# Splitting mixer weights with casting and accumulating transfers instead of GpSimd

## The chip, the cores and the metric

The kernel runs on one core of a Trainium2 chip. The metric is the device time of one execution in microseconds (us); the time before is the median of three runs. The engines are named TensorE (PE; its weight loads PEld), VectorE (DVE), ScalarE (ACT), GpSimd (POOL) and SyncE (SP, which here only issues transfers). Each has its own in-order instruction queue, and they meet at semaphores.

## The reference

Two layers of a network over 256 latent tokens and 256 context tokens of width 1024, all in float32. Each layer is a half-step SwiGLU FFN, a token mixer and another half-step FFN, each with its own modulation, gate and LayerNorm. What matters here is the mixer:

```python
def token_mixer(h, hc, rope, p, ctx_out):
    (ca, cg, lx, lg, gqkv, gz, ga, gb, aq, ak, av, gates) = split_in(h @ p['w_in'])
    ...
    y_conv = conformer_conv(ca, cg, p)
    y_lru, y_lru_c = rglru_branch(lx, lx_c, lg, lg_c, p, ctx_out)
    y_gdn, y_gdn_c = gdn_branch(gqkv, gqkv_c, gz, gz_c, ga, ga_c, gb, gb_c, p, ctx_out)
    ...
    y_att = window_attention(q, k, v, kc, vc, p['att_sink'])

    def merge(y_a, y_b, y_c, y_d, gate_cols):
        gt = jax.nn.sigmoid(gate_cols).reshape(gate_cols.shape[:-1] + (N_BRANCH, D))
        mrg = gt[..., 0, :] * (y_a @ p['proj_conv'])
        mrg = mrg + gt[..., 1, :] * (y_b @ p['proj_lru'])
        mrg = mrg + gt[..., 2, :] * (y_c @ p['proj_gdn'])
        mrg = mrg + gt[..., 3, :] * (y_d @ p['proj_att'])
        return mrg @ p['w_out']
```

In the second (last) layer only the latent tokens are merged, so most of its projections have 256 columns in place of 512.

## The kernel before

Every large product is made of three TensorE products of rounded operands: a float32 value r is split into hi, which is r rounded to the format fp32r, and lo = r - hi, and w x is wh xh + wh xl + wl xh (`mm3`, lines 376 to 381). Weights come from HBM as tiles of 128 partitions by 1024 columns (0.5 MB), and `chunk` (line 98) splits each: SP issues the transfer into one of two buffers `wr`, ScalarE casts it into `wh` (line 120), and VectorE or GpSimd subtracts to make `wl` (line 121). There are three `wh` and three `wl` buffers; some weights go to other slots (F, G, Y, B) instead. In a G slot a weight is two halves with a cast and a subtraction each.

Who subtracts is given by `self.lo`, a string of letters through which successive weights cycle: P is GpSimd, D is VectorE. The mixer is a set of generators (GDN convolution, keys and values, scan, attention, conformer convolution, LRU, merges), and a string of letters per layer, `ORDER`, says which one takes its next step. Three capital letters in that string set `self.lo` (line 36):

```python
LO = {"P": "P", "D": "DP", "X": "D"}
```

In the first mixer P is set for most of the weights and "DP" from the merges on, and after the string `self.lo = "D" if last else "DP"` (line 1322) holds for the last merges and the output projection. In the second mixer P is set after the first letter and D after the string. A projection onto the mixer's inputs (`z`, line 542) takes one weight and 24 matmuls. A merge step (`merge`, line 1269) takes three weights: a projection tile, used in two halves of 12 matmuls, and a gate's tile (24 matmuls) ahead of each half.

The order of instructions on each queue is not the program's alone: the kernel is built by a planner (`schedule_with_timeline_sim=True`) that plays the program through with costs of its own and puts on each queue, by priority, what it thinks is ready. A transfer that GpSimd issues is an instruction in GpSimd's queue, and what is behind it waits until its semaphores allow it.

The lines that the prediction names: 120 and 121 the split of a weight, 127 the split of an activation (subtraction), 868 and 831 the GDN scan's multiplications on GpSimd, 864 and 877 its work on VectorE, 1107 the 31-tap convolution on VectorE, 1047 to 1068 the LRU, 1294 the merge's addition on GpSimd.

Of the kernel before, what the change touches and what calls it, by code (L numbers as in the profile page):

```python
# [12 lines left out]
F32 = mybir.dt.float32  # L13
F32R = mybir.dt.float32r
BF16 = mybir.dt.bfloat16
AF = mybir.ActivationFunctionType
ALU = mybir.AluOpType
P = 128
D = 1024
# [13 lines left out]
    0, 124, 128, 132, 136, 168, 176, 184, 192, 200, 296, 298, 300, 301, 309)  # L33
NEG = -1e30
N_CH = 16
LO = {"P": "P", "D": "DP", "X": "D"}
ORDER = (
    "eggePgegeggXgeggggggPgegggvggvggvggvgggggggaabgggabggzabababzabababllllggababababzababgllablglzbvvvvvccccvvccvccssssssssPssssssDmmllllmmllllsmmmmsmmmmmmmm",
    "gPggggeeeggecgggcgeggggeggccgvgvggvvggggccgagggggbaabgzggggvggabzvabgccggvabbabazbvvvvvzssssslssssssslllllsPssmmlllllsmmmllllmlmmmmmmmmmm",
# [10 lines left out]
class Net:  # L50
# [46 lines left out]

    def chunk(self, src, at=None, raw=None):
        nc = self.nc
        pool_lo = self.lo[self.n_ck % len(self.lo)] == "P"  # L100
        self.n_ck += 1
        if raw is None:
            raw = self.sb.tile([P, 1024], F32, tag="wr", bufs=2, name="wr")
            nc.sync.dma_start(raw, src)
        elif isinstance(raw, str):
            raw = self.slot(raw, name="raw")[:, :1024]
            nc.sync.dma_start(raw, src)
        if at == "G":
            hi, lo = ([self.G(F32R) for _ in range(2)] for _ in range(2))
            parts = [(hi[k], lo[k], raw[:, k * 512:(k + 1) * 512]) for k in range(2)]  # L110
        else:
            if at:
                w = self.slot(at, F32R, name="w" + at)
                hi, lo = w[:, :1024], w[:, 1024:]
            else:
                hi = self.sb.tile([P, 1024], F32R, tag="wh", bufs=3, name="wh")
                lo = self.sb.tile([P, 1024], F32R, tag="wl", bufs=3, name="wl")
            parts = [(hi, lo, raw)]
        for h, l, r in parts:
            nc.scalar.copy(h, r)  # L120
            (nc.gpsimd if pool_lo else nc.vector).tensor_sub(l, r, h.bitcast(F32))  # L121
        return hi, lo

    def split(self, hi, lo, src, pool_lo=True):
# [280 lines left out]
    def ffn(self, l, f, j, tiles, H, fill, after, start=None):  # L405
# [9 lines left out]
        def two(src, at=(None, None)):  # L415
            if lat:
                return self.pair(src, "Y", at)
            return [chunk(src[a], at[a]) for a in range(2)]

        for fi, (m0, m1) in enumerate(F_SPLIT):  # L420
# [48 lines left out]
            if fi < len(F_SPLIT) - 1:  # L469
                for dh in range(2):  # L470
                    ps = {t: self.ps("px" if t == 3 else "pm") for t in tiles}
                    ws = []
                    for i in range(n):
                        i0 = m0 // 2 + i
                        if i == n - 1 and not i % 2:
                            ws.append(chunk(src[dh][i]))
                        elif not i % 2:
                            ws += two(self.t["f2"][l, f, dh, i0:i0 + 2])
                        w = ws[i]
                        for t in tiles:  # L480
                            self.down_mm(ps[t], hid, t, n, i, w)
                        if fill and i % 2:
                            fill.pop(0)()
                    for t in tiles:
                        self.resid(t, dh, ps[t], ALPHA if fi == 0 else 1.0)
            else:
                while fill:
                    fill.pop(0)()
                ws = [[chunk(src[dh][i], at=DOWN_AT[dh][i]) for i in range(n)] for dh in range(2)]


# [41 lines left out]
        else:  # L533
            nc.vector.tensor_add(x, x, t1)

# [1 line left out]

    def z_mm(self, ps, w, H, c):
        for k in range(KD):
# [759 lines left out]
    def mixer(self, l, H, last, after):  # L1299
        nc = self.nc  # L1300
        tiles = (2, 3) if last else (0, 1, 2, 3)
        c = slice(256, 512) if last else slice(0, 512)
        self.vec = self.sb.tile([P, V_N], F32, tag="vec", bufs=1, name="vec")
        with self.tc.issue_after(self.mark):
            nc.scalar.dma_start(self.vec, self.t["vec"][l])
        self.l, self.inv = l, None
        self.ysp = [self.dr.tile([P, 4, 512], F32, tag=f"ysp{b}", bufs=1, name="ysp") for b in range(4)]
        for s in range(2):
            if not (last and s == 0):
                nc.sync.dma_start(self.xspill[s], self.x[s])  # L1310
        self.z_head(l, H, [Z_GK + h for h in range(4)] + [Z_AK if last else Z_GQ])
        S, extra = self.att_z(l, H, last)
        self.conv_init()
        self.gdn_init()
        st = dict(
            g=self.gdn(l, H, last), v=self.gdn_values(l, H, last), s=self.gdn_scan(last),
            e=(f() for f in extra), a=self.att(self.att_scores, S, tiles),
            b=self.att(self.att_values, S, tiles), z=(self.gdn_z(l, H, last, h) for h in range(4)),
            c=(x for i in range(4) for x in self.conv(l, H, last, i)), l=self.lru(l, H, last), m=self.merges(l, H, last, c))
        ws = {}  # L1320
        self.emit(st, ORDER[l], "gvezabclsm")
        self.lo = "D" if last else "DP"
        y = [None, None]
        if last:
            mh = [a.rearrange("p (k t) -> p k t", k=KD) for a in (self.F(F32R), self.F(F32R))]
            spots = SPOT
        else:
            spots = ("F", "F", "F", "F", "F", "G", "G", None)
        self.ju = self.T

        def fetch(n0, n1):
            for n in range(n0, n1):
                ws[n] = self.chunk(self.t["wo"][l, n // 4, n % 4], at=spots[n])

        def conv_out():
            y[0] = self.new_y()
            self.conv_norm(last, y[0])
            yield

        def gdn_out():  # L1340
            y[1] = self.new_y()
            for t in tiles:
                self.gdn_out(t, y[1])
                yield

        done = [0] * 4

        def merged(i):
            done[i] += 1
            if last and done[i] == 2:  # L1350
                self.mh_split(mh, i, c)

        def merge_conv():
            for i in range(4):
                yield from self.merge(l, 0, y[0], H, last, False, i, lambda: merged(i))

        def merge_gdn():
            for i in range(4):
                yield from self.merge(l, 2, y[1], H, last, False, i, lambda: merged(i))

        def fetches():
            for i in range(4 if last else 7):
                fetch(i, i + 1)
                yield

        self.emit(dict(n=conv_out(), o=gdn_out(), c=merge_conv(), g=merge_gdn(), f=fetches()), TAIL[l], "nocgf")
        if not last:
            mh = self.new_h()
            for i in range(4):
                self.mh_split(mh, i, c)  # L1370
        self.x = [None, None]
        for s in range(2):
            if not (last and s == 0):
                self.x[s] = self.Y(name="x")
                nc.sync.dma_start(self.x[s], self.xspill[s])
        self.gate_rows(l, 1, 0.5, (1,) if last else (0, 1))
        self.norm_rows(l, 1)
        fetch(4 if last else 7, 8)

        def mm(t, dh, sums):  # L1380
            ps = self.ps()
            with self.hold():
                for i in range(4):
                    self.wo_mm(ps, mh, t - 2 if last else t, i, ws[4 * dh + i])
            self.resid(t, dh, ps, ALPHA, sums)

        self.out_loop(tiles, mm, after)

    def emit(self, streams, order, rest):
        for ch in order:  # L1390
            if ch in LO:
                self.lo = LO[ch]
            else:
# [165 lines left out]
```

## Time and profile before

| | |
|---|---|
| median of 3 runs | 2820.98 us (2819.75 to 2821.17) |
| profiled execution | span 2816.3 us from first to last instruction, 37869 instructions |
| around the span, to the median | 4.7 us |
| TensorE busy | 2593.8 us, 92% |
| VectorE busy | 1955.0 us, 69% |
| ScalarE busy | 1093.3 us, 39% |
| GpSimd busy | 1008.0 us, 36% |
| moved by transfers | 396.99 MB, 141 GB/s on the mean; transfers issued by GpSimd 0.07 MB |

The profiled execution is one execution, and its own time is given by its span; the runs are timed without that profile. Busy times are of the whole span, and stages with different limits are mixed in them. The mean of a group of instructions mixes undisturbed and stretched ones. "Idle before" names what ended an engine's wait.

### The profile page before, as it was taken

How to read it: one execution, taken by the hardware profiler on the slowest of the kernel's cores; microseconds unless marked ns; L12 is line 12 of the kernel's file. 1: busy time of each engine (PE TensorE's matmuls, PEld its weight loads, DVE VectorE, ACT ScalarE, POOL GpSimd, SP SyncE). 2: the span in 40 equal slices, each digit the busy share in tenths (PEclk: the TensorE clock that was granted, in tenths of full speed). 3: DMA queues.
4: the chain of work that ended last, by engine and by line, in shares of the span. 5: the costliest groups of instructions: out<-in, count | busy, mean ns of one | idle time of the engine just before them, and what ended most of it. 6: DMA issues, size and time to landing. Idle time of an engine off the chain costs nothing.

```text
span 2816.3 us, 37869 instructions
## 1 busy us (share of the span) xinstructions
PE 2593.8 (92%) x14382; PEld 2174.2 (77%) x14382; DVE 1955.0 (69%) x3129; ACT 1093.3 (39%) x1995; POOL 1008.0 (36%) x691
## 2 busy tenths in 40 slices
PE   5999998998898999999999999999979878888898
PEld 3787877776777787878878888888867767688898
DVE  8695966678999834265969467623698898756455
ACT  3322235483332533353222442223536534344443
POOL 4323223222535344433232332323332278731221
PEclk9999999999999999999999999999989989999899
DMA  6554542234422343434545344423222534357353
GB/s 226 191 179 169 201 145 102 69 109 153 140 83 91 113 135 117 164 113 157 181 171 196 102 166 167 149 95 115 91 90 92 156 116 133 105 183 240 135 181 118
DMA packets 162216, 396.99 MB, mean 141 GB/s; under 512 B 28417, under 2 KB 68577, under 8 KB 161265
## 3 DMA queue, kind: packets, MB, share of 16 engines
q1 hardware_dynamic: 158114, 384.55, 40.9%
q10 hardware_dynamic: 3888, 9.96, 1.1%
q8 instruction: 113, 1.85, 0.3%
q14 instruction: 69, 0.57, 0.1%
q0 software_dynamic: 32, 0.07, 0.0%
HBM read 360.92 MB, written 33.60 MB: 140 GB/s over the span
## 4 chain that ended last, share of the span: by engine, by line
PE 34%; DVE 13%; issue 3%; DMA 2%; POOL 2%; ACT 2%; SPq 0%; POOLq 0%; ACTq 0%; DVEq 0%
PE pm L380 10%; PE pm L381 10%; PE pm L379 10%; DVE C L1107 2%; DVE G L572 1%; DVE junk L169 1%; DVE wl L121 1%; DVE G L864 1%; PE px L381 1%; PE px L380 1%; PE px L379 1%; DMA wr<-in_wo_dram 1%; DVE lru L1049 1%; DVE M L781 1%; PE pg L873 0%
## 5 line engine op out<-in xcount | busy, mean ns | idle before, releaser
L379 PE MATMUL pm<-h,wh 128*128 128x512 f32 (+1 forms) x2512 | 895.5, 358 | 36.6 <-ACT h L125 12.8
L381 PE MATMUL pm<-h,wl 128*128 128x512 f32 (+1 forms) x2512 | 890.9, 355 | 16.8 <-DVE wl L121 14.8
L380 PE MATMUL pm<-h,wh 128*128 128x512 f32 (+1 forms) x2512 | 892.0, 355 | 13.0 <-POOL h L127 6.7
L121 POOL TENSOR_TENSOR wl<-wr,wh 128x1024 fp32r<-128x1024 f32 x166 | 419.8, 2530 | 697.6 <-ACT wh L120 649.0
L120 ACT CAST wh<-wr 128x1024 fp32r<-128x1024 f32 x340 | 356.7, 1050 | 785.6 <-PE pm L380 275.2
L379 PEld LDWEIGHTS pm<-h,wh 128*128 128x128 f32 x2512 | 484.0, 193 | 109.1 <-ACT h L125 15.6
L381 PEld LDWEIGHTS pm<-h,wl 128*128 128x128 f32 x2512 | 484.8, 193 | 87.0 <-DVE wl L121 18.8
L380 PEld LDWEIGHTS pm<-h,wh 128*128 128x128 f32 x2512 | 485.1, 193 | 80.9 <-POOL h L127 10.1
L121 DVE TENSOR_TENSOR wl<-wr,wh 128x1024 fp32r<-128x1024 f32 x174 | 243.6, 1400 | 263.0 <-ACT wh L120 261.6
L169 DVE SCALAR_TENSOR_TENSOR junk<-wa,cb 128x1024 bf16<-128x1024 f32 x256 | 358.3, 1442 | 9.2 <-DMA wa<-in_adaw_dram 8.6
L127 POOL TENSOR_TENSOR F<-G,F 128x512 fp32r<-128x512 f32 (+1 forms) x94 | 139.4, 1483 | 426.2 <-ACT F L125 426.1
L1107 DVE SCALAR_TENSOR_TENSOR C<-C,vec 128x482 f32<-128x482 f32 (+29 forms) x240 | 208.2, 867 | 4.1 <-ACT C L1099 0.9
L380 PE MATMUL pm<-wl,F 128*128 128x512 f32 x368 | 145.5, 395 | 0.0
L379 PE MATMUL pm<-wh,F 128*128 128x512 f32 x368 | 145.4, 395 | 0.0
L381 PE MATMUL pm<-wh,F 128*128 128x512 f32 x368 | 144.1, 395 | 0.0
L393 DVE TENSOR_TENSOR G<-G,pm 128x512 f32<-128x512 f32 (+1 forms) x93 | 54.4, 585 | 125.9 <-PE pm L381 118.9
L121 DVE TENSOR_TENSOR wl<-raw,wh 128x1024 fp32r<-128x1024 f32 x61 | 75.0, 1231 | 63.6 <-ACT wh L120 63.6
L125 ACT CAST F<-G 128x512 fp32r<-128x512 f32 (+1 forms) x94 | 50.9, 542 | 154.1 <-DVE G L393 154.1
L868 POOL TENSOR_TENSOR wk<-wk,cd 128x512 f32<-128x512 f32 x56 | 70.8, 1267 | 94.1 <-PE pg L890 75.4
L572 DVE SCALAR_TENSOR_TENSOR G<-pm,vec,G 128x506 f32<-128x506 f32 (+5 forms) x126 | 87.2, 692 | 24.5 <-ACT G L567 22.7
L120 ACT CAST wh<-raw 128x1024 fp32r<-128x1024 f32 x64 | 66.8, 1047 | 88.1 <-PE pm L380 38.8
L1294 POOL TENSOR_TENSOR mrg<-mrg,M 128x512 f32<-128x512 f32 (+1 forms) x48 | 51.9, 1085 | 117.5 <-DVE M L1293 117.5
(408 smaller groups left out, 4493.8 us busy)
## 6 DMA issues: line engine op xcount, KB each, us to landing
wr<-in_f_dram SPq DMA_DIRECT2D x204, 512.0 KB, 3.6
wa<-in_adaw_dram SPq DMA_DIRECT2D x72, 1024.0 KB, 4.9
wr<-in_win_dram SPq DMA_DIRECT2D x132, 512.0 KB, 3.6
raw<-in_f_dram SPq DMA_DIRECT2D x30, 1024.0 KB, 4.9
wr<-in_prj_dram SPq DMA_DIRECT2D x32, 512.0 KB, 3.7
gt<-gsp SPq DMA_DIRECT2D x12, 768.0 KB, 5.2
gsp<-G SPq DMA_DIRECT2D x32, 256.0 KB, 2.7
wr<-in_wo_dram SPq DMA_DIRECT2D x16, 512.0 KB, 3.7
```

Of the source, the lines that this page charges most:

```text
L120: nc.scalar.copy(h, r)
L121: (nc.gpsimd if pool_lo else nc.vector).tensor_sub(l, r, h.bitcast(F32))
L127: eng.tensor_sub(lo, src, hi.bitcast(F32))
L169: nc.vector.scalar_tensor_tensor(junk, w3[:, a], 1.0, self.cb[:, s], op0=ALU.mult, op1=ALU.mult, accum_out=self.modT[l][:, i + a, s:s + 1])
L379: nc.tensor.matmul(ps, wh, xh, start=first, stop=False)
L380: nc.tensor.matmul(ps, wh, xl, start=False, stop=False)
L381: nc.tensor.matmul(ps, wl, xh, start=False, stop=last)
L393: nc.vector.tensor_mul(hf[:, c], sg[:, c], pu[:, c])
L572: nc.vector.scalar_tensor_tensor(acc[:, :, d:], src[:, :, :n - d], w(j), acc[:, :, d:], op0=ALU.mult, op1=ALU.add)
L868: nc.gpsimd.tensor_mul(S(d, n + 1).rearrange("p (h e) -> p h e", h=4), S(d, n).rearrange("p (h e) -> p h e", h=4), gs["cd"][:, d * N_CH + ...
L1107: V.scalar_tensor_tensor(o, x, w(j), o, op0=ALU.mult, op1=ALU.add)
L1294: nc.gpsimd.tensor_add(dst, dst, th[:, c])
```

## The change

Where GpSimd would have subtracted (letter P) in a mixer, the weight now goes the way "A": GpSimd issues a transfer from HBM that casts into `wh` directly, ScalarE writes the negated hi into `wl`, and GpSimd issues a second transfer of the same raw weight from HBM that adds into `wl`, which makes it r - hi. These weights use no `wr` buffer and no transfer by SP. The letters P and D of the order strings now mean "A" and "DA"; the letter P itself stays in use in the FFNs, and for weights that come with a raw tile at hand.

```diff
-LO = {"P": "P", "D": "DP", "X": "D"}
+LO = {"P": "A", "D": "DA", "X": "D"}
...
     def chunk(self, src, at=None, raw=None):
         nc = self.nc
-        pool_lo = self.lo[self.n_ck % len(self.lo)] == "P"
+        kind = self.lo[self.n_ck % len(self.lo)]
         self.n_ck += 1
+        if kind == "A" and raw is None:
+            return self.chunk_dma(src, at)
...
-            (nc.gpsimd if pool_lo else nc.vector).tensor_sub(l, r, h.bitcast(F32))
+            (nc.gpsimd if kind == "P" else nc.vector).tensor_sub(l, r, h.bitcast(F32))
+        return hi, lo
+
+    def chunk_dma(self, src, at):
+        nc = self.nc
+        if at == "G":
+            hi, lo = ([self.G(F32R) for _ in range(2)] for _ in range(2))
+            parts = [(hi[k], lo[k], src[:, k * 512:(k + 1) * 512]) for k in range(2)]
+        else:
+            if at:
+                w = self.slot(at, F32R, name="w" + at)
+                hi, lo = w[:, :1024], w[:, 1024:]
+            else:
+                hi, lo = (self.sb.tile([P, 1024], F32R, tag=t, bufs=3, name=t) for t in ("wh", "wl"))
+            parts = [(hi, lo, src)]
+        for h, l, r in parts:
+            nc.gpsimd.dma_start(h, r)
+            nc.scalar.mul(l, h.bitcast(F32), -1.0)
+            nc.gpsimd.dma_start(l, r, accum_op=ALU.add)
         return hi, lo
...
-        self.lo = "D" if last else "DP"
+        self.lo = "D" if last else "DA"
```

## Rows read from the trace of the kernel before

**Rows 1.** Stretch: length, busy us of PE, PEld, DVE, ACT, POOL, clock, DMA

```profile
406.00:1010.00 604.00, 554.92 (x3275) 448.05 (x3274) 472.60 (x846) 265.99 (x600) 226.86 (x178) 0.96 0.34 109
1010.00:1240.00 230.00, 228.04 (x1031) 186.39 (x1030) 103.55 (x154) 88.91 (x149) 95.31 (x60) 1.00 0.40 130
2005.00:2490.00 485.00, 408.32 (x2977) 354.96 (x2978) 397.34 (x706) 222.83 (x479) 263.81 (x196) 0.94 0.38 120
```

**Rows 2.** The chain of waits, second mixer: start us, us, what

```profile
2078.44 2.51 DVE C L1107
...
2081.56 2.51 DVE C L1107
...
2084.10 0.49 DVE C L1107
```

**Rows 3.** GpSimd's timeline there: start us, us, what

```profile
2078.19 2.48 POOL L121 TENSOR_TENSOR wl<-wr,wh 128x1024 fp32r<-128x1024 f32 x1 [2.67 <-ACT wh L120]
...
2081.22 2.57 POOL L121 TENSOR_TENSOR wl<-wr,wh 128x1024 fp32r<-128x1024 f32 x1
```

**Rows 4.** VectorE's groups by shape, 2005 to 2490 us: busy us, mean ns

```profile
L1107 DVE SCALAR_TENSOR_TENSOR C<-C,vec 128x245 f32<-128x245 f32 x8 | 10.7, 1339 | 0.1
...
L1107 DVE SCALAR_TENSOR_TENSOR C<-C,vec 128x244 f32<-128x244 f32 x8 | 3.7, 465 | 0.1
```

**Rows 5.** VectorE's groups by line, 2005 to 2490 us

```profile
L1107 DVE SCALAR_TENSOR_TENSOR C<-C,vec 128x241 f32<-128x241 f32 (+14 forms) x120 | 92.8, 773 | 1.8
...
L864 DVE TENSOR_TENSOR G<-gt,gcst 128x512 f32<-128x512 f32 x30 | 31.0, 1073 | 0.0
L1049 DVE SCALAR_TENSOR_TENSOR lru<-T,vec,lru 128x506 f32<-128x506 f32 (+2 forms) x24 | 30.8, 1288 | 0.6 <-POOL lru L1047 0.5
```

**Rows 6.** Lines 1107 (500 to 1000 us), 864 and 1049: duration ns min/median/max

```profile
L1107 DVE SCALAR_TENSOR_TENSOR C<-C,vec x120: 704/734/2890, 718.3 to 948.5; 128x482 f32<-128x482 f32 x8, 128x484 f32<-128x484 f32 x8, 128x486 f32<-128x486 f32 x8, 128x488 f32<-128x488 f32 x8
...
L864 DVE TENSOR_TENSOR G<-gt,gcst x60: 674/849/2943, 712.2 to 2454.6; 128x512 f32<-128x512 f32 x60
...
L1049 DVE SCALAR_TENSOR_TENSOR lru<-T,vec,lru x48: 728/746/2855, 676.5 to 2417.9; 128x506 f32<-128x506 f32 x16, 128x508 f32<-128x508 f32 x16, 128x510 f32<-128x510 f32 x16
```

**Rows 7.** VectorE's groups by line, 406 to 1240 us

```profile
L1107 DVE SCALAR_TENSOR_TENSOR C<-C,vec 128x482 f32<-128x482 f32 (+14 forms) x120 | 115.4, 961 | 2.3 <-ACT C L1099 0.9
...
L864 DVE TENSOR_TENSOR G<-gt,gcst 128x512 f32<-128x512 f32 x30 | 28.3, 998 | 1.2 <-DMA gsp<-G 1.2
L1049 DVE SCALAR_TENSOR_TENSOR lru<-T,vec,lru 128x506 f32<-128x506 f32 (+2 forms) x24 | 26.0, 1114 | 2.0 <-POOL lru L1047 2.0
```

**Rows 8.** GpSimd's groups by shape, 2005 to 2490 us

```profile
L121 POOL TENSOR_TENSOR wl<-wr,wh 128x1024 fp32r<-128x1024 f32 x57 | 139.7, 2453 | 146.9 <-ACT wh L120 135.7 <-PE px L1213 6.8 <-PE pg L890 3.3
```

**Rows 9.** The tile ident: GpSimd's only transfer issue, duration ns

```profile
L132 POOL DMA_DIRECT2D ident<-in_ident_dram x1: 735/735/735, 1.2 to 1.2; - x1
```

**Rows 10.** The page's costliest groups: ScalarE's cast of a weight

```profile
L120 ACT CAST wh<-wr 128x1024 fp32r<-128x1024 f32 x340 | 356.7, 1050 | 785.6 <-PE pm L380 275.2
```

**Rows 11.** Who waited for whom, ScalarE, 406 to 1240 us: total, times, longest

```profile
ACT wh L120 <- PE pm L380: 81.5, 29, 7.9
```

**Rows 12.** Transfer issues: count, KB each, median us to landing

```profile
wr<-in_win_dram SPq DMA_DIRECT2D x132, 512.0 KB, 3.6
...
x<-xspill SPq DMA_DIRECT2D x3, 1024.0 KB, 6.7
...
ident<-in_ident_dram POOLq DMA_DIRECT2D x1, 64.0 KB, 5.3
```

**Rows 13.** TensorE's timeline, first mixer: first and last of 12 matmuls

```profile
923.21 0.40 PE L379 MATMUL pm<-y,wh 128*128 128x512 f32 x1
...
925.78 0.40 PE L381 MATMUL pm<-y,wl 128*128 128x512 f32 x1
```

**Rows 14.** TensorE's timeline, second mixer: first and last of 12 matmuls

```profile
2391.10 0.28 PE L379 MATMUL pm<-y,wh 128*128 128x256 f32 x1
...
2392.39 0.28 PE L381 MATMUL pm<-y,wl 128*128 128x256 f32 x1
```

## The prediction

> **What bounds the kernel now.** I read the busy times by stage first, then the chain of waits in the second mixer, then VectorE's groups by shape and by line, then GpSimd's groups and TensorE's timeline. The profiled execution spans 2816.3 us; the three runs have a median of 2820.98 us, 4.7 us more, which I add back at the end as it is. A measurement of this kernel tells 0.2% (5.6 us) from no change.
>
> The stages differ [rows 1]. From 406 to 1010 us (first mixer) TensorE is busy 92% of the time, and 99% from 1010 to 1240 us, where the merges end: there TensorE sets the pace. From 2005 to 2490 us (second mixer, mostly half as many columns) TensorE is busy 84% and VectorE 82%, and the chain runs along VectorE. Its pieces tell why: the same convolution step of line 1107 takes 0.49 us in one place and 2.51 us in the next [rows 2]. The long ones coincide with GpSimd's split of a weight on line 121: two splits begin at 2078.19 and 2081.22 us and take 2.5 us, and two long steps of VectorE begin at 2078.44 and 2081.56 us [rows 2, 3]. While GpSimd reads two operands from SBUF, a VectorE instruction with two operands there stands still. By shape: 245 columns take 1339 ns on average, 244 columns 465 ns [rows 4].
>
> What this costs VectorE, from three lines: in the second mixer L1107 takes 92.8 us for 120 where 120 x 0.465 would be 55.8, so 37 us too much; L864 31.0 where 30 x 0.674 = 20.2, 10.8 too much; L1049 30.8 where 24 x 0.728 = 17.5, 13.3 too much: 61 us [rows 4 to 6]. In the first mixer it is 115.4 against 120 x 0.734 = 88.1, 28.3 against 20.2, and 26.0 against 17.5: 44 us [rows 6, 7]. GpSimd's other work does some of it. The splits of weights are 139.7 of its 263.8 busy us in the second mixer [rows 1, 8], 53%; its other instructions are mostly shorter and hold VectorE less long, so I give the splits 70%: 43 and 31 us of VectorE's time.
>
> **The change, part by part.** The order strings and the alternation in the code give 26 + 28 = 54 weights of the new kind in the first mixer (every second one once the letter D is reached) and all 57 after the first letter P in the second, where the trace has 57 splits [rows 8]. Two of the 54 come in halves, so GpSimd issues 109 x 2 + 2 x 4 = 226 transfers.
>
> On GpSimd a split of 2.45 us goes [rows 8] and two issues come. The only GpSimd issue in the trace took 0.735 us [rows 9], so 1.47 us, and GpSimd is 0.98 us freer per weight. It does not bound; I count nothing. Nor do I for the 111 issues that leave SP's queue, which hides them under transfers.
>
> On ScalarE the cast of 1.05 us [rows 10] becomes a negation of the same size: nothing. But it now waits for the cast's landing, with the tanh, exp and copies of the scan behind it.
>
> Of VectorE's freed 43 us in the second mixer most lie on the path; I take 0.7 of them, since TensorE (84%) is close behind: 30 us. In the first mixer TensorE leads, so a third of 31: 10 us. The gain is 40 us (bounds: 0, if the issues hold VectorE as the splits do, and 74, all of it).
>
> The bytes: 111 x 0.5 MB are read twice, 58 MB more; the transfers' share of the mixers is 0.34 to 0.40 [rows 1], which leaves room, so nothing.
>
> The term that decides is the way from a free buffer to a usable weight. Today the raw weight already lies in one of two buffers of its own, and ScalarE waits for TensorE to give back one of three wh/wl pairs (81.5 us in 29 waits in the first mixer [rows 11]); from there it is 1.05 + 2.45 us, with hand-overs about 4 us. The new transfers write into the pair itself, so nothing can be fetched before it is free, and then come in series: issue 0.74, casting transfer, negation 1.05, issue 0.74, accumulating transfer. The trace has neither kind of transfer. For the cast it has 3.6 us (a weight by SP) below and 5.3 us (the one GpSimd transfer, small, at the start) above [rows 12]; I take 4.5. For the accumulation, which also reads its destination, it has 3.6 us below and 6.7 us for twice the bytes above [rows 12]; I take 5.5, nearer the latter. That is 12.5 us; with 2.5 us for standing in the queues of ScalarE (46% busy) and GpSimd, 15 us. Bounds: 9.7 us, without queues and with 3.6 twice, and 20 us, with both upper ends and more queue.
>
> The Trainium skill's page "DMA: Bandwidth & Descriptors" (section "Anatomy of one DMA — SWDGE (gpsimd) path") gives a GpSimd transfer 2.0 us + bytes / 436 GB/s, an estimate of 3.2 us here, and its page "Collectives: The Full Stack" (section "The bandwidth ceiling: the fold count and why AG ≠ RS ≠ AR") says that an adding transfer is slower because it reads two sources, an estimate of 4.4 us. By these the way would be about 12.6 us and the sum below 2864 us; no row shows such a transfer.
>
> What do the 11 us more cost? A pair is asked for when the third-last weight is done, so two weights' work can hide the way. In the first mixer a matmul of 512 columns goes by every 0.234 us [rows 13], 5.6 us for a weight of 24; in the second one of 256 columns every 0.117 us [rows 14], 2.8 us. In plain runs two weights hide 11 and 5.6 us, and other matmuls lie between. The merges are worse: their order is gate, half the projection (12 matmuls), gate, half the projection, and the projection keeps its pair through both gates. The next merge's first gate gets the pair of the gate before, with only 12 matmuls between: 2.8 us in the first mixer, 1.4 in the second. First mixer: 9 first gates of the new kind x (15 - 2.8) = 110, and 6 second gates behind a first one of the old kind x (2.8 + 15 - 12.4) = 32: 142 us. I take half, 71: TensorE has no idle time to give there, but the planner can let the scan, the attention and the other merge stream fill in. Second mixer: 8 x (15 - 1.4) = 109; TensorE is idle 16%, and a merge takes about 25 us now, above the 22 that the longer way allows, so a third, 36. Together 107 us (bounds: 53 with 9.7 us, 159 with 20 us, 251 if nothing fills in).
>
> The sum: 2816.3 - 40 + 107 = 2883.3 us in span, + 4.7: **2888 us**, 2.4% slower.
>
> **The rivals.** First, the relief wins. If the planner moves other matmuls into every gap, the longer way is hidden and VectorE's freed time shows. For it speak the 16% of idle TensorE and a mean gap between weights above what three pairs need (485 us / 57 = 8.5 us, against (15 + 2.8) / 3 = 5.9). Against it: weights come in bunches, and a TensorE at 92 to 99% has nothing to hide them with in the first mixer. Time: 2821 - 40 = 2781 us, down to 2750. It decides once the way is under some 8 us.
>
> Second, GpSimd's queue stands still. An accumulating issue waits for ScalarE, which waits for the cast's landing; behind it on GpSimd stand the scan's multiplications (L868, L831), the LRU's and the merge's additions, and the scan waits for those. If each of some 30 scan steps waits 4 us and the transfers are at their upper ends, that is 2821 + 120 + 159 - 40 = 3060 us. For it: one in-order queue with 226 new issues. Against it: the planner places an issue where it thinks the data is there.
>
> Third, VectorE holds up the issues. If GpSimd can't write its descriptors while VectorE works (82% busy in the second mixer [rows 1]), each issue is late by up to an instruction of 0.5 to 1 us, the way becomes some 16.5 us, and the cost rises by 9/2 + 6/2 + 8/3 = 10 us for each of the 1.5: 2903 us. The Trainium skill's page "SBUF — State Buffer" (section "SBUF: two separate sides") states this for VectorE's two-port modes; no row shows it.
>
> Fourth, nothing to measure: stalls near their lower bound (53) against a relief near 50, within 6 us of 2821.
>
> **How the numbers follow.** Forecast 0.47 (its own range 2835 to 2940), relief 0.26, queue 0.13, issues held up 0.07, nothing 0.07. Faster 0.26, same 0.07, slower 0.47 + 0.13 + 0.07 = 0.67. The range goes from 2770, inside the relief's, to 3040, short of the standing queue's; that leaves 0.2 out at most.
>
> **What would show it.** Right: GpSimd's line 121 almost gone from both mixers and some 226 issues in its place, line 1107 in the second mixer near 56 us, accumulating landings of 5 to 6 us, TensorE waiting for a gate's weight from 870 us on, and a lower granted clock where it waits (0.94 in the second mixer now, at 84% busy [rows 1]). Wrong: if landings are 3 us or less and TensorE's share rises, the relief has won; if GpSimd's waits for ScalarE grow and the scan's L868 comes late, the queue has. A casting transfer of over 10 us would break the sum altogether.

## The result and the profile after

The change makes the kernel slower: 2899.64 us (median of 4 runs, 2889.48 to 2909.81) against 2820.36 us before (4 runs), a ratio of 1.0275 (95% interval 1.0244 to 1.0306), 79 us. The forecast was 2888 us. The profiled execution spans 2890.8 us. In it, lines from 122 on stand 20 lower than before: the three matmuls are L399 to L401, the convolution step is L1127, the scan's two-operand step L884. L139 issues the casting transfer, L140 is the negation, L141 issues the accumulating transfer.

First, what the change was to remove. VectorE's groups in the second mixer, by shape and then by line (2042 to 2536 us, busy us and mean ns):

```profile
L1127 DVE SCALAR_TENSOR_TENSOR C<-C,vec 128x245 f32<-128x245 f32 x8 | 3.8, 470 | 0.1
...
L1127 DVE SCALAR_TENSOR_TENSOR C<-C,vec 128x241 f32<-128x241 f32 (+14 forms) x120 | 60.6, 505 | 3.3 <-ACT C L1119 1.3
L884 DVE TENSOR_TENSOR G<-gt,gcst 128x512 f32<-128x512 f32 x30 | 33.7, 1163 | 4.3 <-DMA gt<-gsp 4.3
L1069 DVE SCALAR_TENSOR_TENSOR lru<-T,vec,lru 128x506 f32<-128x506 f32 (+2 forms) x24 | 22.7, 948 | 0.1
```

The step of 245 columns took 1339 ns beside GpSimd's splits [rows 4] and takes 470 now; the line's 92.8 us [rows 5] are 60.6. Lines 1127 and 1069 got faster, L884 did not (31.0 us before): each of its steps of over 0.9 us lies beside a computation that GpSimd still does, the scan's L888 and L851 above all, and none beside an issue alone. So the relief came.

Second, the way of a weight. The transfer issues of the mixers' weights (count, KB each, median us to landing):

```profile
wh<-in_win_dram POOLq DMA_DIRECT2D x92, 512.0 KB, 4.8
wl<-in_win_dram POOLq DMA_DIRECT2D x92, 512.0 KB, 5.7
...
wh<-in_prj_dram POOLq DMA_DIRECT2D x14, 512.0 KB, 4.2
wl<-in_prj_dram POOLq DMA_DIRECT2D x14, 512.0 KB, 6.0
```

The durations of the casting issue on GpSimd (ns min/median/max):

```profile
L139 POOL DMA_DIRECT2D wh<-in_win_dram x92: 527/572/911, 480.7 to 2560.3; - x92
```

And of the accumulating one:

```profile
L141 POOL DMA_DIRECT2D wl<-in_win_dram x92: 827/880/1182, 488.6 to 2566.0; - x92
```

The mean of all landing times of L141 less the mean of all starts of L139 is taken as the mean way from a free pair to a usable weight: 12.6 us in the first mixer, 14.4 in the second. It is a lower bound, since GpSimd stood waiting for TensorE to give back the pair ahead of some 66 of the 113 casting issues; ahead of the others the pair may have been free for a while.

Third, where the time went. I bound each mixer by the end of the normalization that precedes it and of the one that ends it (line 371 before, 391 after), so the columns of a row cover the same work. The columns are length, busy us (and instructions) of PE, PEld, DVE, ACT and POOL, granted clock, DMA share and GB/s. Before, first and second mixer:

```profile
450.80:1256.70 805.90, 755.18 (x4182) 612.05 (x4180) 559.08 (x957) 344.93 (x730) 316.51 (x233) 0.97 0.36 116
2009.60:2606.00 596.40, 506.22 (x3690) 447.91 (x3689) 467.45 (x809) 273.75 (x563) 280.07 (x216) 0.94 0.44 139
```

After:

```profile
450.50:1287.40 836.90, 767.63 (x4182) 618.02 (x4181) 496.79 (x957) 344.18 (x730) 258.55 (x289) 0.96 0.56 146
2046.30:2680.00 633.70, 529.47 (x3691) 464.08 (x3689) 396.72 (x810) 274.94 (x563) 211.00 (x273) 0.90 0.69 178
```

The first mixer is 31.0 us longer, the second 37.3; of the span's 74.5 that leaves 6.2, most of it in the feed-forward network behind the first mixer. VectorE's busy time fell by 62.3 and 70.7 us. TensorE's grew by 12.4 and 23.3 us for the same number of matmuls: in the second mixer the granted clock fell from 0.94 to 0.90.

One weight shows the way and its after-effect. GpSimd's timeline in the second mixer (start us, us, engine and line, then the idle time before):

```profile
2443.52 0.58 POOL L139 DMA_DIRECT2D wh<-in_win_dram  x1
...
2447.40 1.04 POOL L888 TENSOR_TENSOR wk<-wk,cd 128x512 f32<-128x512 f32 x1 [1.79 <-PE pg L910]
2450.23 2.43 POOL L851 TENSOR_TENSOR rx<-rx,gcst 128x128 f32<-128x128 f32 x3 [1.79 <-PE pg L854]
2452.61 0.89 POOL L141 DMA_DIRECT2D wl<-in_win_dram  x1
```

ScalarE's timeline, the negation between the two issues:

```profile
2447.62 1.05 ACT L140 ACTIVATE wl<-wh 128x1024 fp32r<-128x1024 f32 x1
```

The chain of waits there (start us, us, what):

```profile
2448.80 0.12 PE pm L400
...
2452.61 7.84 DMA wl<-in_win_dram
2460.45 0.04 issue
2460.49 0.58 PE pm L401
2461.07 0.21 PE pm L399
```

And 2.4 us further on in that chain:

```profile
2463.42 0.21 PE pm L401
2463.64 0.12 PE pm L399
```

The cast is issued at 2443.52, the negation ends at 2448.67, but the accumulating issue starts 3.9 us later, because GpSimd first waits 1.79 us for TensorE and then works for 2.4 us on the scan's L851. The landing comes at 2460.45, 16.9 us after the first issue. TensorE waited 5.7 us for it, and then its matmuls of 256 columns go by every 0.21 us instead of 0.12 until 2463.6: the lower of its two clock levels, 1.2 instead of 2.4 GHz. The stretches around it, columns as for the mixers:

```profile
2455.00:2461.00 6.00, 0.51 (x2) 0.51 (x3) 5.35 (x9) 0.57 (x2) 1.79 (x3) 0.64 1.06 229
2461.00:2466.00 5.00, 5.00 (x36) 5.00 (x35) 0.78 (x2) 1.25 (x3) 0.56 (x1) 0.75 0.27 95
2466.00:2475.00 9.00, 8.93 (x74) 5.70 (x73) 2.37 (x7) 7.82 (x13) 6.13 (x9) 1.00 0.97 186
```

The granted clock is 0.75 in the 5 us behind the wait, with TensorE busy throughout, and 1.00 after that. A wait of 5.7 us cost more than itself. The DMA engines were full while this transfer was under way (share 1.06; a transfer is counted whole where it starts), and it took 7.84 us where the median is 5.7. Whether the load made it late was not tested.

Who waited in the second mixer (total us, times, longest), TensorE:

```profile
PE pm L401 <- DMA wl<-in_win_dram: 19.1, 9, 5.7
...
PE pm L399 <- DMA wh<-in_win_dram: 10.1, 6, 3.2
...
PE pm L401 <- DMA wl<-in_prj_dram: 3.0, 2, 1.8
```

GpSimd:

```profile
POOL wh L139 <- PE pm L401: 106.3, 30, 14.1
POOL mrg L1314 <- DVE M L1313: 73.0, 18, 9.7
POOL wl L141 <- ACT wl L140: 68.5, 22, 9.4
```

Some 32 us of TensorE's waiting bears the new transfers' names (with 3.0 for projections); the rest has to be found by experiment. By these rows GpSimd waits 175 us for pairs and negations (228 us with everything that its two issues waited for), which looks like the rival of the standing queue.

### The profile page after: what moved, and what is told of

The parts are those of the page before. It is cut to its first block, busy times and chain, and to the rows that moved or that the text cites. A ratio compares the mean times of both kernels' runs of the same rounds, so it can differ in the third digit from the quotient of the medians.

```text
span 2890.8 us, 38026 instructions
## 1 busy us (share of the span) xinstructions
PE 2633.6 (91%) x14382; PEld 2200.0 (76%) x14382; DVE 1820.1 (63%) x3129; ACT 1094.1 (38%) x1995; POOL 881.4 (30%) x804
## 3 DMA queue, kind: packets, MB, share of 16 engines
q0 software_dynamic: 32576, 116.47, 18.5%
## 4 chain that ended last, share of the span: by engine, by line
PE 37%; issue 8%; DMA 4%; DVE 4%; POOL 2%; ACT 1%; POOLq 0%; SPq 0%; ACTq 0%; DVEq 0%
PE pm L401 11%; PE pm L400 11%; PE pm L399 11%; PE pg L893 1%; DMA wh<-in_win_dram 1%; PE px L401 1%; PE px L400 1%; PE px L399 1%; DMA wl<-in_win_dram 1%; POOL wl L141 1%; DVE G L884 1%; POOL wh L139 1%; DMA wr<-in_wo_dram 1%; POOL h L147 0%; DMA wl<-in_prj_dram 0%
## 5 line engine op out<-in xcount | busy, mean ns | idle before, releaser
L399 PE MATMUL pm<-h,wh 128*128 128x512 f32 (+1 forms) x2512 | 901.4, 361 | 39.1 <-ACT h L145 14.6
L401 PE MATMUL pm<-h,wl 128*128 128x512 f32 (+1 forms) x2512 | 898.1, 359 | 41.0 <-DMA wl<-in_win_dram 26.9
L401 PEld LDWEIGHTS pm<-h,wl 128*128 128x128 f32 x2512 | 489.3, 195 | 116.3 <-DMA wl<-in_win_dram 33.5
L399 PEld LDWEIGHTS pm<-h,wh 128*128 128x128 f32 x2512 | 489.4, 196 | 114.2 <-ACT h L145 17.3
L400 PEld LDWEIGHTS pm<-h,wh 128*128 128x128 f32 x2512 | 490.4, 195 | 80.8 <-POOL h L147 10.2
L122 ACT CAST wh<-wr 128x1024 fp32r<-128x1024 f32 x234 | 245.6, 1050 | 626.2 <-PE pm L400 213.5
L123 POOL TENSOR_TENSOR wl<-wr,wh 128x1024 fp32r<-128x1024 f32 x60 | 161.8, 2697 | 354.4 <-ACT wh L122 354.4
L140 ACT ACTIVATE wl<-wh 128x1024 fp32r<-128x1024 f32 x106 | 112.0, 1060 | 261.7 <-DMA wh<-in_win_dram 202.4
L141 POOL DMA_DIRECT2D wl<-in_win_dram x92 | 81.2, 886 | 275.5 <-ACT wl L140 186.2
L1127 DVE SCALAR_TENSOR_TENSOR C<-C,vec 128x482 f32<-128x482 f32 (+29 forms) x240 | 157.4, 656 | 6.4 <-ACT C L1119 3.0
L399 PE MATMUL pm<-wh,F 128*128 128x512 f32 x368 | 145.4, 395 | 0.0
L401 PE MATMUL pm<-wh,F 128*128 128x512 f32 x368 | 144.1, 395 | 0.0
L139 POOL DMA_DIRECT2D wh<-in_win_dram x92 | 57.5, 625 | 246.0 <-PE pm L401 223.9
L592 DVE SCALAR_TENSOR_TENSOR G<-pm,vec,G 128x506 f32<-128x506 f32 (+5 forms) x126 | 87.3, 693 | 24.8 <-ACT G L587 23.3
```

The source lines that it names most:

```text
L123: (nc.gpsimd if kind == "P" else nc.vector).tensor_sub(l, r, h.bitcast(F32))
L139: nc.gpsimd.dma_start(h, r)
L140: nc.scalar.mul(l, h.bitcast(F32), -1.0)
L141: nc.gpsimd.dma_start(l, r, accum_op=ALU.add)
L399: nc.tensor.matmul(ps, wh, xh, start=first, stop=False)
L400: nc.tensor.matmul(ps, wh, xl, start=False, stop=False)
```

## The experiments

All are compared with the kernel before, run on the same chip beside them. This table has the medians of all runs and the lengths of the mixers as bounded above, of one profiled execution each. The planner orders every kernel's queues anew, and no run shows what that alone moves: the two relief kernels have the same median and differ by 7.8 us in the second mixer, so a difference of that size between two rows tells little.

| kernel | us | ratio to before (95%) | first mixer | second mixer |
|---|---|---|---|---|
| before | 2820 to 2823 | 1 | 805.9 | 596.4 |
| the change | 2899.64 | 1.0275 (1.0244 to 1.0306) | 836.9 | 633.7 |
| relief alone | 2759.12 | 0.9783 (0.9767 to 0.9799) | 789.9 | 549.8 |
| relief, GpSimd's queue standing | 2758.04 | 0.9778 (0.9756 to 0.9800) | 790.5 | 542.0 |
| relief, transfers to scratch | 3184.65 | 1.1288 (1.1269 to 1.1307) | | |
| no accumulating transfer | 2787.30 | 0.9883 (0.9866 to 0.9900) | 808.4 | 561.3 |
| raw weight by SP, accumulating transfer | 2819.77 | 0.9987 (0.9971 to 1.0003) | 822.2 | 580.3 |
| change in the first mixer alone | 2853.15 | 1.0117 (1.0091 to 1.0142) | 836.7 | 592.8 |
| change in the second mixer alone | 2859.21 | 1.0140 (1.0118 to 1.0161) | 807.3 | 638.3 |
| change in the merges alone | 2880.12 | 1.0196 (1.0170 to 1.0222) | 835.1 | 631.7 |
| change in all but the merges | 2859.93 | 1.0133 (1.0111 to 1.0154) | 831.8 | 617.0 |
| the change with a fourth pair | 2877.76 | 1.0198 (1.0167 to 1.0228) | 838.6 | 619.7 |
| VectorE subtracts | 2785.10 | 0.9878 (0.9859 to 0.9897) | 789.9 | 579.2 |
| VectorE first mixer, two ways in turn in the second | 2791.88 | 0.9892 (0.9874 to 0.9911) | 794.5 | 585.3 |

### Relief alone

```diff
             nc.scalar.copy(h, r)
-            (nc.gpsimd if pool_lo else nc.vector).tensor_sub(l, r, h.bitcast(F32))
+            if pool_lo and self.mix:
+                nc.scalar.mul(l, h.bitcast(F32), -1.0)
+            else:
+                (nc.gpsimd if pool_lo else nc.vector).tensor_sub(l, r, h.bitcast(F32))
```

This is against the kernel before; `self.mix` is true in the mixers.

> The way of before (raw weight by SP into a buffer of its own, cast by ScalarE), but where GpSimd subtracted, ScalarE writes minus hi as lo: the lo half leaves out the raw weight. No transfer by GpSimd, no split by it in the mixers. Longer-way theory as forecast (relief 40 us, way 4 us): 2781 us, bounds 2747 to 2821. Rival, that the relief is nearer the time that VectorE got back in the trace after (62 + 72 us in the mixers): about 2750. Then the longer way cost not 107 us but about 79 + 70 = 150.

Measured 2759.12 us, 62 below before, nearer to the rival's 71 than to the forecast's 40. Its two mixers:

```profile
446.20:1236.10 789.90, 751.54 (x4181) 610.04 (x4179) 500.58 (x956) 395.20 (x785) 185.19 (x177) 0.98 0.37 119
1992.30:2542.10 549.80, 494.57 (x3690) 439.49 (x3689) 389.74 (x809) 325.70 (x620) 134.74 (x159) 0.96 0.48 151
```

The mixers are 16.0 and 46.6 us shorter, with 58.5 and 77.7 us less of VectorE: 27% and 60% of it reached the end. A part is not relief: from the start of the cast to a usable weight it is 2.5 and 2.7 us on average here, and was 4.0 and 4.6 us before where GpSimd split. So, against this kernel, the longer way of the change costs 2899.64 - 2759.12 = 140.5 us; in the profiled executions it is 137.2, of which 47.0 are in the first mixer and 83.9 in the second. In the second it is TensorE idle for 49.0 us more (length less busy time: 55.2 against 104.2) and busy 34.9 us more for the same 3690 matmuls, at a granted clock of 0.90 instead of 0.96.

### GpSimd's queue standing, without transfers

```diff
             if pool_lo and self.mix:
+                nc.gpsimd.memset(l[:, :4].bitcast(F32), 0.0)
                 nc.scalar.mul(l, h.bitcast(F32), -1.0)
+                nc.gpsimd.tensor_copy(l[:, :4], h[:, :4].bitcast(F32))
```

This is against relief alone.

> As the kernel with relief alone, plus two tiny instructions on GpSimd per weight in the order of the change's two issues: a memset of 4 columns of lo, which waits for the free pair and which the negation waits for, and a copy of 4 columns behind the negation. GpSimd's queue stands still at the same places as in the change, without transfers. Lo leaves out the raw weight. Longer-way theory: within 10 us of relief alone. Standing-queue theory: at least 60 us above relief alone.

Measured 2758.04 us, 1 us from relief alone, well inside the intervals. GpSimd's waits in the second mixer of this kernel:

```profile
POOL wl L122 <- PE pm L386: 137.2, 40, 18.8
POOL wl L124 <- ACT wl L123: 73.3, 33, 4.6
```

It stands at a pair or a negation for 210 us there, about as long as in the change (175 us by the same two rows, 228 in all), and nothing is lost. The standing queue as such is not the cause. What this kernel lacks is the wait for a landing between the two instructions: the second one waits 4.6 us at most, in the change 9.4.

### The transfers into scratch

```diff
                 nc.scalar.mul(l, h.bitcast(F32), -1.0)
+                g = [self.dr.tile([P, 1040], F32R, tag=f"scr{i}", bufs=4, name=f"scr{i}") for i in range(2)]
...
+                nc.gpsimd.dma_start(g[0][:, :n], s)
+                nc.gpsimd.dma_start(g[1][:, :n], s, accum_op=ALU.add)
```

This too is against relief alone.

> As the kernel with relief alone, plus the change's two GpSimd transfers of each weight (casting and accumulating), written to scratch in HBM, which no engine waits for: the issues and the bytes without the way. Lo leaves out the raw weight. Longer-way theory: within 10 us of relief alone. Rival, that the load of the transfers or the issues' time on GpSimd costs the time: 50 us or more above relief alone.

Measured 3184.65 us, but this run tells nothing on the question. The landings of this kernel's scratch transfers:

```profile
scr<-in_win_dram POOLq DMA_DIRECT2D x184, 512.0 KB, 16.9
```

Its first 480 us (columns as for the mixers above):

```profile
0.00:480.00 480.00, 83.67 (x235) 56.80 (x235) 73.36 (x134) 40.64 (x63) 181.09 (x239) 0.62 1.06 273
```

No weight held these transfers back, and they run from the start to 505 us; there the DMA engines are full, TensorE works for 84 of 480 us, and the first mixer begins 414 us late. From there to the end it is 46 us faster than before. The question of bytes went to the next but one.

### Without the accumulating transfer

```diff
             nc.gpsimd.dma_start(h, r)
             nc.scalar.mul(l, h.bitcast(F32), -1.0)
-            nc.gpsimd.dma_start(l, r, accum_op=ALU.add)
```

This and the kernels that follow are against the change, where nothing else is said.

> The change without its accumulating transfer (lo is minus hi, without the raw weight): from a free pair to a usable weight about 0.7 + 4.7 + 1.05 + hand-overs = 7.5 us instead of 14, half the transfers. Longer-way theory with its 107 us for 11 us more (9.7 us a microsecond): 3.5 x 9.7 = 34, so 2820 - 40 + 34 = 2815 us; if the relief is 75 and the way 150, about 2795. Standing-queue theory (GpSimd still waits for each pair, 264 us in the trace after): about 2860.

Measured 2787.30 us, 28 above relief alone, 8 below the longer-way theory's second figure (2795, with the larger relief) and far below the standing queue's 2860. Its mixers:

```profile
449.30:1257.70 808.40, 755.55 (x4182) 615.10 (x4181) 501.67 (x957) 344.69 (x730) 214.30 (x233) 0.97 0.37 116
2013.40:2574.70 561.30, 500.26 (x3692) 446.60 (x3690) 392.29 (x809) 274.74 (x563) 160.71 (x216) 0.94 0.48 147
```

The way is 5.7 and 5.6 us on average; it costs 18.5 us in the first mixer and 11.5 in the second, against relief alone.

### Raw weight by SP, only the accumulation by GpSimd

```diff
         if kind == "A" and raw is None:
-            return self.chunk_dma(src, at)
+            acc, kind = src, "A"
...
             nc.scalar.copy(h, r)
-            (nc.gpsimd if kind == "P" else nc.vector).tensor_sub(l, r, h.bitcast(F32))
+            if acc is not None:
+                nc.scalar.mul(l, h.bitcast(F32), -1.0)
+                s = acc if len(parts) == 1 else acc[:, 512 * (h is hi[1]):][:, :512]
+                nc.gpsimd.dma_start(l, s, accum_op=ALU.add)
+            else:
+                (nc.gpsimd if kind == "P" else nc.vector).tensor_sub(l, r, h.bitcast(F32))
```

> Raw weight by SP into its own buffer as before, cast and negation by ScalarE, and only the raw weight's second arrival as the change has it: an accumulating transfer from HBM into lo. The whole computation. The bytes are the change's; from a free pair to a usable weight it is 1.05 + 1.05 + 0.9 + 5.7 = 8.7 us, with hand-overs 9.2, and GpSimd does not wait for the pair. Longer-way theory, between the kernel without the accumulating transfer (some 6.5 us, 2787) and the change (14 us, 2900): about 2828 us. Rival, that the bytes or the transfers on GpSimd cost the time: 2870 or more. Rival, that GpSimd standing at the pair costs it: about 2780.

Measured 2819.77 us, no different from before, 61 above relief alone and 80 below the change. Its mixers:

```profile
449.70:1271.90 822.20, 768.89 (x4181) 625.11 (x4179) 510.99 (x957) 395.33 (x787) 230.01 (x233) 0.95 0.56 148
2030.00:2610.30 580.30, 508.48 (x3691) 449.99 (x3689) 392.26 (x810) 327.39 (x620) 178.49 (x216) 0.94 0.73 194
```

And its accumulating transfers:

```profile
wl<-in_win_dram POOLq DMA_DIRECT2D x92, 512.0 KB, 6.4
```

The DMA share is that of the change (0.56 and 0.73 against 0.56 and 0.69) and the accumulating transfers land even later (6.4 us against 5.7), yet 80 us are gone with the way, which is 9.6 and 10.9 us on average here, from the start of a weight's cast to the accumulating landing. So the bytes are not what costs these 80 us. Nor do the 61 us above relief alone point to them: for each microsecond of way they come to 4.5 us in the first mixer and 3.7 in the second, no more than in the kernel without the accumulating transfer (5.7 and 3.9), which reads each weight once. The transfers that GpSimd issues are half of the change's here, so their number is not tested by this kernel. The longer-way theory had 2828, 8 us off.

### One mixer at a time

```diff
-        if kind == "A" and raw is None:
+        if kind == "A" and raw is None and self.l == 0:
...
-            (nc.gpsimd if kind == "P" else nc.vector).tensor_sub(l, r, h.bitcast(F32))
+            (nc.gpsimd if kind in "PA" else nc.vector).tensor_sub(l, r, h.bitcast(F32))
```

The other kernel has `self.l == 1` there. Weights that the condition leaves out are split by GpSimd as before.

> The change in the first mixer alone, the second as before. By the stages of the two traces (31 us in the first mixer, 6 in the network after it): 2821 + 37 = 2858 us. By the forecast's sum (71 - 10): 2882. If the mixers' losses are not their own (a later stage pays): another number, and the two kernels with one mixer each do not add up to 79.

> The change in the second mixer alone, the first as before. By the stages of the two traces: 2821 + 37 = 2858 us. By the forecast's sum (36 - 30): 2827.

Measured 2853.15 and 2859.21 us: 30 and 37 above before. The stages of the traces had 37 for each, the forecast's sum 61 and 6. The two together make 67 of the 79 us; I leave the other 12 open (6 of them stand in the network behind the first mixer, which is 4 us longer in the first kernel too).

### The merges alone, and all but the merges

```diff
-        if kind == "A" and raw is None:
+        if kind == "A" and raw is None and self.mg:
```

`self.mg` is true while a merge asks for its projection or a gate; the other kernel has `not self.mg`.

> The change for the weights of the merges alone (gates and projections); the other weights of the mixers that GpSimd split are split by it as before. Forecast: the way costs its 107 us here, less the merges' share of the relief (some 40 of 111 weights, 15 us of 40): 2821 + 92 = 2913 us. By the stages of the two traces (nothing lost in the first mixer's merges, 32 us in the second's): 2853.

> The change for all weights but those of the merges. Forecast: two weights' work hides the way, so only the relief's share shows: 2821 - 25 = 2796 us. By the stages of the two traces: 2821 + 79 - 32 = 2868.

Measured 2880.12 and 2859.93 us, 59 and 38 above before. The trace counts 45 weights in the merges and 66 elsewhere: 1.3 us a weight against 0.6. Merges are the worse place, as forecast, but the plain runs do not hide the way: there the forecast was 2796. And the parts don't add up: in the first mixer either one alone makes it nearly as long (835.1, 831.8) as both (836.9). It may be that what is late in one part is partly made up in the next; no run shows it.

### A fourth pair

```diff
+                self.n_dma += 1
+                tags = (("wr", 2),) * 2 if self.lo == "A" and self.n_dma % 4 == 3 and (self.l == 0 or 54 + 12 < self.n_dma < 54 + 36) else (("wh", 3), ("wl", 3))
-                hi, lo = (self.sb.tile([P, 1024], F32R, tag=t, bufs=3, name=t) for t in ("wh", "wl"))
+                hi, lo = (self.sb.tile([P, 1024], F32R, tag=t, bufs=n, name=t) for t, n in tags)
```

> The change, and in two stretches (the 26 weights up to the first that alternate, in the first mixer, and 24 in the middle of the second) every fourth new weight takes the two raw-weight buffers, which lie unused there, as its pair: four pairs in place of three. Transfers, bytes, queue and issues are the change's. Longer-way theory, that it costs because no pair is free early enough: 25 us less than the change, about 2875 (2850 to 2890). Rival, that the transfers themselves or GpSimd's queue cost: 2900, as the change.

Measured 2877.76 us, 22 less than the change, with the same transfers on the same queue, and by the intervals of the two ratios clear of it. Its second mixer:

```profile
2044.80:2664.50 619.70, 518.88 (x3691) 457.74 (x3689) 402.58 (x810) 273.40 (x563) 211.18 (x273) 0.92 0.70 182
```

The profiled executions differ by 15.5 us, 14.0 of them in the second mixer. The way itself is not shorter (13.0 and 14.6 us), which speaks for the free pair as what counts there. The first mixer is not shorter (838.6): that part of the theory is not shown by this run.

### VectorE subtracts, and a mixture

```diff
-LO = {"P": "P", "D": "DP", "X": "D"}
+LO = {"P": "D", "D": "D", "X": "D"}
...
-        self.lo = "D" if last else "DP"
+        self.lo = "D"
```

This is against the kernel before.

> Nothing by transfers: VectorE subtracts where GpSimd did, in all mixer weights. The whole computation. It removes the same splits from GpSimd, and gives VectorE 111 x 1.38 = 153 us of work against the 134 us that it got back in the trace after. If VectorE's time sets the pace of the second mixer: within 15 us of before (2821). If it is the way from a free pair to a usable weight that counts, which is now 1.05 + 1.38 and shorter by a us: 2790. If VectorE's own order suffers (a split stands in front of the scan): 2850.

Measured 2785.10 us, 1.2% faster than before: the way is no longer than before (3.3 and 2.9 us on average from cast to split, against the 4.0 and 4.6 of GpSimd's splits), and VectorE's busy time in the second mixer is 452.05 us against 467.45, although it does 57 more splits:

```profile
1994.50:2573.70 579.20, 506.50 (x3691) 448.93 (x3689) 452.05 (x866) 275.06 (x563) 150.66 (x159) 0.93 0.46 143
```

VectorE's work other than splits of weights falls from 419.0 to 335.2 us there: some 84 us of what it was busy with before was standing beside GpSimd's splits (relief alone has 78 us less of VectorE). The time is that of the second case, the shorter way (2790); but VectorE's own time fell too, so the run does not tell the two apart. The mixture applied the SP way with the accumulating transfer to every second weight of the second mixer, on top of VectorE in the first:

```diff
-LO = {"P": "A", "D": "DA", "X": "D"}
+LO = {"P": "AD", "D": "DA", "X": "D"}
...
-        if kind == "A" and raw is None:
+        if kind == "A" and raw is None and self.l == 1:
+            acc, kind = src, "A"
...
```

The rest is as with the raw weight by SP.

> VectorE subtracts in the first mixer (as in the kernel in which it subtracts everywhere: 15 us gained there); in the second mixer every second weight goes VectorE's way and the others the way with the raw weight by SP and the accumulating transfer. The whole computation. If the cost of the longer way falls faster than in proportion when only every second weight has it (in the second mixer 12, 30 and 84 us for ways of 5, 10 and 12 to 14 us), the second mixer gains 22 us instead of 17: about 2778 us. If each way's cost is its own share: 17 us there, 2785. If two ways in turn hold the pairs out of step: 2795 or more.

Measured 2791.88 us, nearest to the last case (2795 or more) and not better than VectorE alone; its second mixer is 11.1 us shorter than before's, VectorE's 17.2. The version to keep is VectorE's.

## Why the prediction was right, and where it was not

**The way: right.** Forecast 15 us (9.7 to 20), measured 12.6 and 14.4. Its terms were near: landing of the cast 4.2 to 4.8 us for 4.5, of the accumulation 5.7 to 6.0 for 5.5, issues 0.57 and 0.88 for 0.74, negation 1.06. The Trainium skill's two pages, "DMA: Bandwidth & Descriptors" (section "Anatomy of one DMA — SWDGE (gpsimd) path") and "Collectives: The Full Stack" (section "The bandwidth ceiling: the fold count and why AG ≠ RS ≠ AR"), led to estimates of 3.2 and 4.4 us for the landings; the trace has 4.8 and 5.7, so here the rows of before were the better guide, while the order of the two is as the second page has it.

**The relief: mechanism right, too small.** Forecast 40 us, measured 62 by the kernel with relief alone, which also has the way shorter than before by 1.5 and 1.9 us. By the costs of a microsecond in the table below that is some 15 us, an estimate, which leaves 47 for the relief itself; then the longer way, counted from before as the forecast counts it, costs not 140.5 but some 125 us. The shares that I took for what reaches the end, a third and 0.7, measured 27% and 60%, with those 15 us in them. The term that was off is VectorE's freed time: 31 and 43 us from three lines, where all of VectorE's lines together gave back 62.3 and 70.7 in the change. Taking three lines for the engine's sum lost about half of it.

**The price of the longer way: mechanism right, both mixers mis-sized.** Forecast 107 us, measured 140.5 against relief alone, as 47.0 (forecast 71) and 83.9 (forecast 36). By the length of the way, against relief alone:

| kernel | mean way, first and second | cost, first and second |
|---|---|---|
| relief alone | 2.5, 2.7 us | 0, 0 |
| no accumulating transfer | 5.7, 5.6 | 18.5, 11.5 |
| raw by SP, accumulating | 9.6, 10.9 | 32.3, 30.5 |
| the change | 12.6, 14.4 | 47.0, 83.9 |

In the first mixer each microsecond of way costs about 4.5 to 5.7 us all along, where the forecast had 71 / 11 = 6.5. In the second it is 3.7 to 3.9 up to 11 us, close to the forecast's 36 / 11 = 3.3, and then some 15 for each of the last 3.5. The last two kernels differ in more than the length of the way (who fetches the raw weight, and where GpSimd stands), so this steep end is not shown to be the way's alone. The sum had no term for what the waits do to the clock: TensorE's busy time in the second mixer goes 494.6, 500.3, 508.5, 529.5 us along the four kernels for the same matmuls. I had named a lower clock as a sign, and left its price out. This error (+33) and that of the relief (-22) have opposite signs, and so have those of the two mixers (-24 and +48): that 2888 came within 12 us is luck, though the mechanism and the direction are not.

**The merges: half right.** They cost twice as much a weight, but the step by which two weights' work hides the way in plain runs failed: all but the merges cost 38 us where 25 less was forecast. And TensorE's waits for a gate's weight from 870 us on are few: in the whole first mixer 11 us are put down to the new landings. There the lateness goes through the order of the work instead; which step passes it on is left open.

**Counted at nothing: confirmed, as far as the runs go.** ScalarE is as busy as before (344.93 and 344.18 us in the first mixer, 273.75 and 274.94 in the second), and the bytes do not show (raw weight by SP, with the change's DMA share), unless in single late landings such as the one at 2460.45. Nor do the transfers hold VectorE's convolution: line 1127 takes 505 ns on average in the change's second mixer and, as line 1110, 511 in relief alone, where GpSimd issues none:

```profile
L1110 DVE SCALAR_TENSOR_TENSOR C<-C,vec 128x241 f32<-128x241 f32 (+14 forms) x120 | 61.4, 511 | 2.4 <-ACT C L1102 0.6
```

**The rivals.** Relief wins: it does with a way of 5.7 us (2787), not at 12 to 14, as its condition of 8 us said; at about 10 it is even (2820). GpSimd's queue standing still: not the cause as a whole, by 210 us of standing that cost nothing; but single issues do come late behind the scan (3.9 us at 2448), and that is part of the way. VectorE holding up the issues: not seen. Of the change's casting issues, 57 lie beside work of VectorE for over 90% of their time and 29 for under 10%, and both kinds take 577 ns in the median; of the accumulating ones, 45 and 31 do, with 886 and 887. From issue to landing the means are 5.2 against 5.0 us and 6.3 against 6.2. The rule of the Trainium skill's page "SBUF — State Buffer" (section "SBUF: two separate sides") on VectorE's two-port modes is not shown by any run here.

## What to carry to other kernels

A prefetch that lands in the operand's own buffer starts only when that buffer is free; count the whole way from free buffer to usable operand and set it against what the other buffers hide, before counting what the engines save. An engine's freed time is to be summed over all its lines in the stage, not read from a few, and a wait put on TensorE can cost twice, as idle time and as matmuls at the lower clock (49.0 and 34.9 us in the second mixer here). Where two engines stand in each other's way, it can be cheaper to give the work to the one that was held up: in the second mixer here VectorE alone did 57 more splits in 15 us less of busy time.

## What the runs showed that was not expected

- GpSimd could stand for 210 us of a 542 us stage at other engines' semaphores without any loss of time.
- With raw weights by SP beside the accumulating transfers, the latter landed after 6.4 us instead of 5.7, and with scratch in HBM as the target, the DMA engines being full, after 16.9.
- After a wait of 5.7 us TensorE's matmuls took 0.21 us instead of 0.12 for about 3 us.
- A casting issue on GpSimd took 572 ns, an accumulating one of the same shape 880.
